# Turned tiles, first weight loads, exponentials and state rows: four small moves in the order of a one-core decoder step

## The chip, the cores and the metric

The kernel runs on one core of a Trainium2 chip. A core has five engines with instruction streams of their own: TensorE (PE in the profile, with its weight loads as PEld), VectorE (DVE), ScalarE (ACT), GpSimd (POOL) and SyncE (SP, which here only issues transfers). They meet through semaphores: an instruction waits until another engine or a transfer has counted a semaphore up. On-chip memory is SBUF, and the matmul results go to PSUM, which has eight banks here. The metric is the device time of one launch in microseconds. Over three runs the kernel before takes 994.75 us (median; 994.54 to 995.33). Smaller is better.

## What is computed

One step of a decoder layer over a prompt of 512 tokens and eight samples of four tokens (544 token columns together), with a model width of 1024:

```python
h = rmsnorm(x, norm_mix_pre)
xr, q, k, v, g = split(h @ w_in)              # 1024 x 4608
A = rg_lru(causal_conv4(xr))                  # r, i = sigmoid(block-diagonal products)
                                              # a = exp(log_a), mult = sqrt(1 - a*a), linear scan
B = sliding_window_attention(q, k, v)         # 8 heads, 2 kv heads, sinks, relative bias
m = (sigmoid(gA) * (A @ w_lru_o) + sigmoid(gB) * (B @ w_attn_o)) @ w_out
x = x + rmsnorm(m, norm_mix_post)
u = causal_conv3(rmsnorm(x, norm_ffn_pre) @ w_up)          # 1024 x 8192
x = x + rmsnorm((gelu(u_gate) * u_val) @ w_down, norm_ffn_post)
```

Besides x it returns the states: the last recurrent rows, the last keys and values, and the last two rows of `h @ w_up` for the prompt and for each sample (`p_ffn_conv` and `s_ffn_conv`).

## The kernel before, in words

Activations lie turned: channels on the 128 partitions, tokens along the free axis, in eight tiles `k` of 128 channels. A product in single precision is made of three matmuls on operands split into a high and a low part (`hH`, `hL` and `wh`, `wl`): high by high, low by high, high by low. The 544 columns are done in two halves, 256 and 288 columns wide (`HALF`). PE runs one long list of such products in the order of the program text; ACT and DVE run an order written out by hand too. What is not a product (splits of weights, gates, scans, norms, outgoing rows) hangs on a clock of the program: `now[0]` counts a tick for each product step, `start_at(t, generator)` puts side work on a tick, `last` and `late` hold work that is queued at the end of a tick or in the next one. In the second part of the kernel (up and down projections) `slot()` does the same in steps of half a unit.

**The start (L377 to L497).** SP issues the first loads in the order of the text: the first token tiles with the two halves of the first weight tile (L384 to L387), the second weight tile (`wload(1)`), the small `relx` and `ohp`, the token tile 2, the third weight tile (`wload(2)`), token tiles 3 and 4, and the fourth and fifth weight tiles (L388 to L398). Each weight tile is 512 KB. `turn_a(z)` (L467) turns the first 256 token columns of channel tiles 4z to 4z+3 by TensorE transposes into PSUM; `hsplit` makes `hH` of them on ACT and `hL` on DVE; `first_mm` feeds them to the first product. A PSUM bank has room for two such turned tiles of 256 columns. Before the change a bank holds the neighbours 2kk and 2kk+1, and the loop takes the tiles in the order 0, 2, 1, 3, 4, 6, 5, 7 (L480). `keep_a` (L504) copies the turned tiles into SBUF later, `norms` (L554) puts these copies on their ticks, `turn_b` turns the other 288 columns, and `roots` and `spread_roots` make the row `rep` of reciprocal roots.

**The mixer's ticks (L79 to L81, used around L1045 to L1115).** For each of the eight recurrent channel tiles, `GATES` names the tick of the gate products and their sigmoids (`rg`, `ig`), `EXPS` the tick of a Tanh and an Exp (`th`, then `rg` at L994) and `SCANS` that of the scan. The attention gates `ga` get their sigmoids (`gate_later`, L1091) from tick GATES[0] + c + 1 on. A weight split is an ACT copy of 512 columns (`wh_...`, L283) and a DVE subtraction (`wl_...`, L290). How many weights ahead of its product a step splits depends on its tick against `GATES[3]` and `GATES[7]` (the argument `look`, L1109 and L1113). Channels 4 to 7 have ticks 73 to 76 in GATES, and L1111 decides which of the gates `gl` have their sigmoid late.

**The end (L1714 to L1930).** The last eighth of the down projection (four F tiles, group `QL`) works on the second column half in `for c in range(8): down(QL, c, 1, ...)` (L1892). Each such tile is 12 matmuls of 288 columns into one of three PSUM banks (`PM`), then a DVE addition into `ft` (L1815), a square on ACT (`sq_sum`, `sq_ft` in the profile, L1180) and a DVE addition into `acc`; the last square goes to `sq7`. At c = 5 ACT makes a warming Sqrt, which loads the table of that function (L1895). After the eight, PE takes held tiles of the group before, on the first column half; between the first and the second of them `stats` multiplies `acc` and `sq7` with ones (`pst_o`, six and six matmuls of one column). `x1_again` (L1716) turns a saved token tile back in four pieces (`px`), which ACT copies into `xtok`. `ffn_states` (L1731) turns the rows of the ffn state: eight transposes into `pfs` and `pfp`, an ACT copy of each into `ffn_rows_s` and `ffn_rows_p` (L1741, L1742), and a POOL transfer of each to the output; this twice, one time unit (two slots) apart. It starts three units after the plan's eighth tile from the end, `x1_again` one unit after it, with its first turned piece at four.

**The shared buffers.** `S(...)` draws from a pool of 53 SBUF tiles (`S_BUFS`, L46). A tile that has been read for the last time gives its buffer to a later one, and the first writer of that later one waits for that last reading; where this is a transfer to the output, it waits until the transfer has landed. When the last eight down tiles run, these S tiles are read until the end: `ft` (8), `x1r` (8, read in `finish_b`), the high and low F tiles 24 to 31 (16), the split weights `dl` (16: four k, two kk, high and low), and, once written, `xtok` (4): 52 in all. The rows of the ffn state (four tiles of S) come beside them.

The lines that set the state rows' tiles and their place:

```python
            o1, o2 = S(f"ffn_rows_s{kk}"), S(f"ffn_rows_p{kk}")
            act.copy(o1[:, 0:512], px)
            act.copy(o2[:16, 0:512], py[:16, :])
            pool.dma_start(out=os_[:, kk * 512:(kk + 1) * 512], in_=o1[:, 0:512])
...
            start_at(now[0] + 1, x1_again())
            start_at(now[0] + 3, ffn_states())
```

Of the kernel before, what the change touches and what calls it, by code (L numbers as in the profile page):

```python
# [17 lines left out]
P = 128  # L18
D = 1024
KD = D // P  # L20
# [55 lines left out]
KEEP = 3  # L76
FILL = 1
TURNED = 8
GATES = (51, 53, 55, 57, 73, 74, 75, 76)  # L79
EXPS = (58, 59, 60, 61, 78, 79, 80, 81)  # L80
SCANS = (62, 63, 65, 67, 82, 83, 85, 86)  # L81


def _bucket(d):
# [39 lines left out]
def hawk_step(ctx, tc, I, O):  # L124
    nc = tc.nc
    act, dve, pool, pe = nc.scalar, nc.vector, nc.gpsimd, nc.tensor
# [28 lines left out]
    def PX(name):  # L155
        return psx.tile([P, 512], F32, tag="aux", name=name)
# [24 lines left out]
    side, now, serial, late, last, mids, after, taps = [], [0], [0], [], [], [], [], []  # L181

    def start_at(t, gen):
        serial[0] += 1
        side.append([t, serial[0], gen])
# [34 lines left out]
    ident = keep.tile([P, P], F32, name="ident")  # L220
# [7 lines left out]
    def wsrc(key):  # L228
        kind = key[0]
        if kind in ("wr", "wi"):  # L230
            return I["lru_" + kind][0, 4 * key[1]:4 * key[1] + 4].rearrange("n c d -> c n d")
        w = {"in": w_in, "lo": I["w_lru_o"][0], "ao": I["w_attn_o"][0], "out": I["w_out"][0]}[kind]
        c = key[-1]
        return w[:, c * P:(c + 1) * P].rearrange("(k p) n -> p k n", p=P)
# [13 lines left out]
    def wname(i):  # L248
        return "_".join(str(z) for z in order[i])

    def wload(i):
        key = order[i]
        raw = wraw[i] = rp.tile([P, KD, P], F32, tag="raw", name="raw_" + wname(i))
        if key[0] == "wg":
            for z, nme in enumerate(("lru_wr", "lru_wi")):
                nc.sync.dma_start(out=raw[:, 4 * z:4 * z + 4, :],
                                  in_=I[nme][0, 4 * key[1]:4 * key[1] + 4].rearrange("n c d -> c n d"))
        else:
            nc.sync.dma_start(out=raw, in_=wsrc(key))
# [11 lines left out]
    def wsplit_hi(un, eng=None):  # L271
        i, u = un // 2, un % 2
        hl = []
        for x in "hl":
            if order[i] in in_slots:
                t_ = S(f"w{x}{u}_{wname(i)}", F32R)[:, 0:512]
                t_ = t_.rearrange("p (k n) -> p k n", k=4)
            else:
                t_ = wp.tile([P, 4, P], F32R, tag="w", name=f"w{x}{u}_{wname(i)}")
            hl.append(t_)  # L280
        raw = wraw[i][:, 4 * u:4 * u + 4, :]
        if eng is None:
            act.activation(hl[0], raw, AF.Copy)  # L283
        else:
            eng.tensor_copy(hl[0], raw)
        wunits[un] = hl
        return raw, hl
# [89 lines left out]
    def xload(i, halves=(0, 1)):  # L377
        t0, n, src = TOK[i]
        for z in halves:
            xt[i, z] = S(f"x{i}_{z}")  # L380
            nc.sync.dma_start(out=xt[i, z][:n, 0:512], in_=src[:, 512 * z:512 * z + 512])

    raw0 = wraw[0] = rp.tile([P, KD, P], F32, tag="raw", name="raw_" + wname(0))
    for z in range(2):  # L384
        xload(0, (z,))
        xload(1, (z,))
        nc.sync.dma_start(out=raw0[:, 4 * z:4 * z + 4, :], in_=wsrc(order[0])[:, 4 * z:4 * z + 4, :])  # L387
    wload(1)  # L388
    relx = cp.tile([NBK, NH], F32, name="relx")
    nc.sync.dma_start(out=relx, in_=I["rel_bias"])  # L390
    ohp = T("ohp")[:NBK, 0:WIN]
    nc.sync.dma_start(out=ohp, in_=I["c_ohp"])
    xload(2)
    wload(2)
    xload(3)
    xload(4)
    wload(3)
    wload(4)  # L398
    for r, nme in ((8, "norm_mix_post"), (16, "norm_ffn_pre"), (24, "norm_ffn_post")):
        nc.sync.dma_start(out=rows_a[r:r + 8, :], in_=I[nme].rearrange("o (k p) -> (o k) p", p=P))  # L400
# [46 lines left out]
    def xtile(i, k):  # L447
        n = TOK[i][1]
        return xt[i, k // 4][:n, (k % 4) * P:(k % 4 + 1) * P]

    def hsplit(k, a, ps):
        g = pv[:, G_PRE + k:G_PRE + k + 1]
        act.activation(h.get(k, a, 0), ps, AF.Copy, scale=g)
        stt(h.get(k, a, 1), ps, g, f32(h.get(k, a, 0)), ALU.mult, ALU.subtract)
# [4 lines left out]
    u0, u1 = wclaim(2)  # L459
    first_ps = PM("pm_first")  # L460

    def first_mm(k, i0, i1, start=False, stop=False):
        mm(first_ps[:, :256], wunits[k // 4][i0][:, k % 4, :], h.get(k, 0, i1), start, stop)

    ps_ta = []

    def turn_a(z):  # L467
        for kk in (2 * z, 2 * z + 1):
            ps_ta.append(PX(f"ps_ta{kk}"))
            for q in range(4):  # L470
                pe.transpose(ps_ta[-1][:, q * P:(q + 1) * P], xtile(q % 2, 2 * kk + q // 2), ident)

    def first_low(z):
        for k in range(4 * z, 4 * z + 4):
            first_mm(k, 1, 0, stop=k == KD - 1)

    turn_a(0)
    for z in range(FILL):
        dummy(z)
    ks = (0, 2, 1, 3, 4, 6, 5, 7)  # L480
    for q, k in enumerate(ks):
        if q in (0, 4):
            raw, hl = wsplit_hi((u0, u1)[q // 4], eng=dve)
        hsplit(k, 0, ps_ta[k // 2][:, k % 2 * 256:k % 2 * 256 + 256])
        if q in (0, 4):
            wsplit_lo(raw, hl, eng=pool)
        first_mm(k, 0, 0, start=q == 0)
        if q not in (0, 4):
            first_mm(ks[q - 1], 0, 1)
        if q == 2:  # L490
            turn_a(1)
        if q == 3:
            first_mm(k, 0, 1)
            first_low(0)
    first_mm(ks[-1], 0, 1)
    first_low(1)
    xsquare(1, 1, False)  # L497

    xn = [S(f"xn{k}") for k in range(KD)]
# [2 lines left out]
    tb = []  # L502

    def keep_a(k):  # L504
        act.copy(xn[k][:, 0:256], ps_ta[k // 2][:, k % 2 * 256:k % 2 * 256 + 256])

    def keep_b(k, ps):
        (dve.tensor_copy if k % 4 > 1 else act.copy)(xn[k][:, 256:NT], ps[:, :288])
# [45 lines left out]
    def norms():  # L554
        xsquare(0, 1, True)
        yield from roots(0, 2)
        yield
        last.extend(lambda k=k: keep_a(k) for k in range(6))
        last.append(lambda: xsquares(2))
        yield  # L560
        turn_b(range(4))
        last.extend(lambda k=k: keep_a(k) for k in (6, 7))
        yield
        turn_b(range(4, KD))
        last.extend(lambda i=i: xsquares(i) for i in (3, 4))
        yield
        yield from roots(2, 5)
        dve.tensor_scalar(rq, ss[:, 1, 0:4], SCALE, None, ALU.mult)
# [488 lines left out]
    for c in range(8):  # L1057
        start_at(GATES[c], gates(c))
        start_at(EXPS[c], lru_exp(c))
        start_at(SCANS[c], lru_scan(c))  # L1060

# [32 lines left out]
    for c in range(8):  # L1094
        for a in range(2):
            step(("in", 28 + c), h, a, gate_done(sg, c, "ga", True), look=1 if now[0] + 1 >= GATES[0] else 2)
        start_at(GATES[0] + c + 1, once(gate_later, sg, c))
        for a in range(2):
            step(("in", c), h, a, lambda a, ps, c=c: xr_done(c, a, ps), look=1 if now[0] + 1 >= GATES[0] else 2)

# [6 lines left out]
    for c in range(8):  # L1107
        for a in range(2):
            step(("ao", c), A, a, ao_done(c), look=1 if now[0] + 1 <= GATES[3] + 2 else 2)  # L1109
    for c in range(8):  # L1110
        raw = 75 + 2 * c > GATES[7] + 1 and c < 7  # L1111
        for a in range(2):
            step(("in", 20 + c), h, a, gate_done(gl, c, "gl", raw), look=1 if now[0] + 1 <= GATES[7] + 2 else 2)  # L1113
        if raw:
            start_at(SCANS[7] + c - 1, once(gate_later, gl, c))  # L1115
    start_at(now[0] + 8, lru_states())
# [614 lines left out]
    def ffn_states():  # L1731
        os_ = O["s_ffn_conv"].rearrange("o b i (m n) -> (o b i m) n", n=D)
        op = O["p_ffn_conv"].rearrange("o b i (m n) -> (o b i m) n", n=D)
        for kk in range(2):
            px = PX(f"pfs{kk}")
            py = PX(f"pfp{kk}")
            for j in range(4):
                pe.transpose(px[:, j * P:(j + 1) * P], sfT[:, 4 * kk + j].rearrange("p r m -> p (r m)"), ident)
                pe.transpose(py[:16, j * P:(j + 1) * P], stage_p[:, 4 * kk + j].rearrange("p r m -> p (r m)"), ident)
# [4 lines that stand above are left out]
            pool.dma_start(out=op[:, kk * 512:(kk + 1) * 512], in_=o2[:16, 0:512])  # L1744
            yield
# [17 lines left out]
    for i, x in enumerate(plan):  # L1763
        more[0] = min(4, max(0, i - len(plan) + LASTS))
        if x[0] == "s":
            pair(*x[1:])
            slot()
        elif x[0] == "q":
            plain(*x)
            slot(x[3])  # L1770
        else:
            _, q, c, a = x
            down(q, c, a, down_done(q, c))
            slot(a)
        if i == len(plan) - 8:
            start_at(now[0] + 1, x1_again())
            start_at(now[0] + 3, ffn_states())

    yp, ys = O["y_p"][0], O["y_s"].rearrange("b t d -> (b t) d")
    sq7 = {}  # L1780
# [194 lines left out]
```

## Time and profile before

| | value |
|---|---|
| median of three runs | 994.75 us (994.54 to 995.33) |
| the profiled execution's own time | 994.97 us |
| its span, first to last instruction | 993.2 us |
| PE busy | 983.9 us, 99% of the span |
| DVE busy | 746.6 us, 75% |
| ACT busy | 566.5 us, 57% |
| POOL busy | 160.4 us, 16% |
| mean granted TensorE clock | 0.998 |

A row of the timeline reads: start in us from the span's beginning, duration, engine, line of the program, operation, output from input, shape, count of neighbours put together, and in brackets the idle time of that engine before it with what ended it. The table of waits lists, by engine, what was waited for, the sum in us, how often, and the longest. PE's matmuls overlap: one of 256 columns is listed with 0.28 us, while the next one starts sooner than that, so times on PE are read from start to start.

### The profile page before, as it was taken

To read this page: it belongs to the slowest core of one execution; us is meant where nothing else is said; L and a number is where in the kernel's file an instruction comes from. 1 tells how busy PE (TensorE), PEld (TensorE's weight loads), DVE (VectorE), ACT (ScalarE), POOL (GpSimd) and SP (SyncE) were. 2 spreads that over 40 slices of the span, in tenths; PEclk is the share of its full clock that TensorE was granted. 3 is DMA by queue.
4 is the path that set the end of the run, shared out by engine and by line. 5 is a ranking of instruction groups with operands and counts; after the bars stand their busy time and mean duration, and the time that the engine had idled before them with its cause. 6 is when DMAs were issued, how large, how long until landed. Compare 5 with 4: busy or idle time off the path is not lost.

```text
span 993.2 us, 20120 instructions
## 1 busy us (share of the span) xinstructions
PE 983.9 (99%) x7783; PEld 972.7 (98%) x7783; DVE 746.6 (75%) x1609; ACT 566.5 (57%) x1362; POOL 160.4 (16%) x269
## 2 busy tenths in 40 slices
PE   9999999999999999999999999999999999999997
PEld 8999999999999999999999999999999999999996
DVE  5777677766948655589776788888888888888766
ACT  6544433468557535556776655555655555556652
POOL 2062000001504441210001010101010101011004
PEclk9999999999999999999999999999999999999999
DMA  7765222332322535236147676777777777768612
GB/s 209 185 218 185 68 86 86 107 86 80 91 85 86 189 104 144 64 112 196 41 117 165 154 160 160 159 161 158 162 156 163 156 163 156 164 147 204 196 47 90
DMA packets 210999, 135.62 MB, mean 137 GB/s; under 512 B 8845, under 2 KB 197021, under 8 KB 210872
## 3 DMA queue, kind: packets, MB, share of 16 engines
q1 hardware_dynamic: 198920, 112.72, 40.1%
q0 software_dynamic: 11920, 19.59, 11.9%
q10 hardware_dynamic: 64, 2.04, 0.5%
q8 instruction: 61, 1.00, 0.4%
q14 instruction: 34, 0.28, 0.1%
HBM read 111.78 MB, written 11.37 MB: 124 GB/s over the span
## 4 chain that ended last, share of the span: by engine, by line
PE 93%; ACT 2%; DVE 2%; DMA 1%; issue 0%; SPq 0%; DVEq 0%; ACTq 0%
PE pmin L165 21%; PE pmdn L165 17%; PE pux L1524 16%; PE puy L1524 8%; PE pq L1524 6%; PE pmout L165 5%; PE pmlo L165 5%; PE puz L1524 4%; PE pmao L165 4%; DMA raw_in<-in_w_in_dram 1%; PE psc L165 1%; PE pvp L165 1%; PE pg L165 1%; PE ptok L165 1%; PE pt L817 1%
## 5 line engine op out<-in xcount | busy, mean ns | idle before, releaser
L165 PE MATMUL pmin<-hH,wh_in 128*128 128x256 f32 (+1 forms) x568 | 165.2, 293 | 0.2 <-ACT wh_in L283 0.2
L165 PE MATMUL pmin<-hL,wh_in 128*128 128x256 f32 (+1 forms) x568 | 162.8, 289 | 0.0
L165 PE MATMUL pmin<-hH,wl_in 128*128 128x256 f32 (+1 forms) x568 | 158.7, 287 | 0.0
L165 PE MATMUL pmdn<-fH,wh_dn 128*128 128x256 f32 (+1 forms) x448 | 129.2, 288 | 0.2 <-DVE ft L174 0.2
L165 PE MATMUL pmdn<-fL,wh_dn 128*128 128x256 f32 (+1 forms) x448 | 129.0, 288 | 0.0
L165 PE MATMUL pmdn<-fH,wl_dn 128*128 128x256 f32 (+1 forms) x448 | 128.9, 288 | 0.0
L177 DVE SCALAR_TENSOR_TENSOR uc<-u,fv,uc 128x560 f32<-128x560 f32 x128 | 102.0, 797 | 13.3 <-ACT uc L1555 13.2
L165 PEld LDWEIGHTS pmin<-hH,wh_in 128*128 128x128 f32 x568 | 106.9, 188 | 1.9 <-issue 1.2
L165 PEld LDWEIGHTS pmin<-hL,wh_in 128*128 128x128 f32 x568 | 107.1, 189 | 0.1
L165 PEld LDWEIGHTS pmin<-hH,wl_in 128*128 128x128 f32 x568 | 105.0, 188 | 0.2 <-issue 0.2
L165 PEld LDWEIGHTS pmdn<-fH,wh_dn 128*128 128x128 f32 x448 | 84.3, 188 | 0.6 <-issue 0.6
L165 PEld LDWEIGHTS pmdn<-fH,wl_dn 128*128 128x128 f32 x448 | 84.4, 188 | 0.0
L165 PEld LDWEIGHTS pmdn<-fL,wh_dn 128*128 128x128 f32 x448 | 84.3, 188 | 0.0
L1650 ACT COPY u<-pux 128x272 f32<-128x272 f32 x52 | 20.1, 387 | 83.9 <-PE pux L1524 83.8
L168 DVE TENSOR_TENSOR u<-puy,u 128x240 f32<-128x240 f32 (+2 forms) x78 | 24.6, 344 | 49.7 <-PE puy L1524 32.7
L283 ACT ACTIVATE wh_in<-raw_in 128x512 fp32r<-128x512 f32 x70 | 42.8, 628 | 29.8 <-issue 12.1
L174 DVE TENSOR_TENSOR ft<-ft,pmdn 128x256 f32<-128x256 f32 (+1 forms) x104 | 45.2, 436 | 17.1 <-PE pmdn L165 16.6
L290 DVE TENSOR_TENSOR wl_in<-raw_in,wh_in 128x512 fp32r<-128x512 f32 x70 | 48.1, 697 | 1.3 <-ACT wh_in L283 1.2
L1555 ACT ACTIVATE uc<-u,fv 128x560 f32<-128x560 f32 x64 | 48.2, 755 | 0.0
L1450 POOL DMA_DIRECT2D raw_up_s<-raw_up_s x26 | 22.7, 872 | 102.0 <-DMA raw_up_s<-raw_up__7496 4.7
L168 DVE TENSOR_TENSOR wl_dn<-raw_dn,wh_dn 128x512 fp32r<-128x512 f32 x56 | 38.4, 685 | 0.0
L165 PE MATMUL pmout<-mH,wh_out 128*128 128x272 f32 x128 | 37.4, 292 | 0.0
(779 smaller groups left out, 3390.0 us busy)
## 6 DMA issues: line engine op xcount, KB each, us to landing
raw_in<-in_w_in_dram SPq DMA_DIRECT2D x35, 512.0 KB
raw_dn<-in_w_down_dram SPq DMA_DIRECT2D x56, 256.0 KB
raw_up_s<-in_w_up_dram SPq DMA_DIRECT2D x25, 512.0 KB
raw_up_s<-raw_up_s POOLq DMA_DIRECT2D x26, 256.0 KB, 5.6
raw_ao<-in_w_attn_o_dram SPq DMA_DIRECT2D x8, 512.0 KB
raw_lo<-in_w_lru_o_dram SPq DMA_DIRECT2D x8, 512.0 KB
raw_out<-in_w_out_dram SPq DMA_DIRECT2D x8, 512.0 KB
xdram<-xn POOLq DMA_DIRECT2D x8, 272.0 KB, 7.5
```

Of the source, the lines that this page charges most:

```text
L165: pe.matmul(out, l, r, start=start, stop=stop)
L168: dve.tensor_tensor(out=out, in0=a, in1=b, op=ALU.subtract)
L174: dve.tensor_tensor(out=out, in0=a, in1=b, op=ALU.add)
L177: dve.scalar_tensor_tensor(out=out, in0=a, scalar=s_, in1=b, op0=op0, op1=op1)
L283: act.activation(hl[0], raw, AF.Copy)
L290: (eng or dve).tensor_tensor(out=hl[1], in0=raw, in1=f32(hl[0]), op=ALU.subtract)
L817: pe.transpose(pt[:, (2 * ch + j) * P:(2 * ch + j + 1) * P], s3[:, j, ch * P:(ch + 1) * P], ident)
L1450: pool.dma_start(out=w["p4"], in_=w["p2"], accum_op=ALU.add)
L1524: pe.matmul(ps[:, :HN], w, x, start=start and k == 0 and i == 0, stop=stop and k == 3 and i == 2, skip_group_check=True)
L1555: act.activation(yt[j][:, 0:FLATU], u[:, 0:FLATU], AF.Copy, scale=fv[:, j:j + 1])
L1650: act.copy(e[nm_], z)
```

## The change

Four parts. First, a PSUM bank of the first turned columns now holds the channel tiles k and k+4, so that the four banks are all begun by the first turn and completed by the second; the loop takes the tiles in plain order, and the first low product of a tile is queued after the second turn. The copies in `norms` are taken in the order 0, 4, 1, 5, 2, 6, and then 3, 7. Second, the third weight tile is loaded ahead of `relx` and `ohp`, and the fourth ahead of token tiles 2, 3 and 4. Third, the exponentials of the first four recurrent channel tiles come at ticks 60 to 63 instead of 58 to 61, their scans at 64, 65, 67, 69 instead of 62, 63, 65, 67, and the gates of the last four one tick earlier, with the test for `raw` adjusted so that it picks the same tiles. Fourth, the ffn state's rows start five time units after the marked tile instead of three, which is four slots later.

```diff
-GATES = (51, 53, 55, 57, 73, 74, 75, 76)
-EXPS = (58, 59, 60, 61, 78, 79, 80, 81)
-SCANS = (62, 63, 65, 67, 82, 83, 85, 86)
+GATES = (51, 53, 55, 57, 72, 73, 74, 75)
+EXPS = (60, 61, 62, 63, 78, 79, 80, 81)
+SCANS = (64, 65, 67, 69, 82, 83, 85, 86)
...
     wload(1)
+    wload(2)
     relx = cp.tile([NBK, NH], F32, name="relx")
     nc.sync.dma_start(out=relx, in_=I["rel_bias"])
     ohp = T("ohp")[:NBK, 0:WIN]
     nc.sync.dma_start(out=ohp, in_=I["c_ohp"])
-    xload(2)
-    wload(2)
-    xload(3)
-    xload(4)
     wload(3)
+    for i in (2, 3, 4):
+        xload(i)
     wload(4)
...
     def turn_a(z):
-        for kk in (2 * z, 2 * z + 1):
-            ps_ta.append(PX(f"ps_ta{kk}"))
-            for q in range(4):
-                pe.transpose(ps_ta[-1][:, q * P:(q + 1) * P], xtile(q % 2, 2 * kk + q // 2), ident)
+        for k in range(4 * z, 4 * z + 4):
+            if not z:
+                ps_ta.append(PX(f"ps_ta{k}"))
+            for q in range(2):
+                pe.transpose(turned_a(k)[:, q * P:(q + 1) * P], xtile(q, k), ident)
+
+    def turned_a(k):
+        return ps_ta[k % 4][:, k // 4 * 256:k // 4 * 256 + 256]
...
-    ks = (0, 2, 1, 3, 4, 6, 5, 7)
-    for q, k in enumerate(ks):
-        if q in (0, 4):
-            raw, hl = wsplit_hi((u0, u1)[q // 4], eng=dve)
-        hsplit(k, 0, ps_ta[k // 2][:, k % 2 * 256:k % 2 * 256 + 256])
-        if q in (0, 4):
+    for k in range(KD):
+        if k % 4 == 0:
+            raw, hl = wsplit_hi((u0, u1)[k // 4], eng=dve)
+        hsplit(k, 0, turned_a(k))
+        if k % 4 == 0:
             wsplit_lo(raw, hl, eng=pool)
-        first_mm(k, 0, 0, start=q == 0)
-        if q not in (0, 4):
-            first_mm(ks[q - 1], 0, 1)
-        if q == 2:
+        first_mm(k, 0, 0, start=k == 0)
+        if k == 3:
             turn_a(1)
-        if q == 3:
+        if k % 4:
+            first_mm(k - 1, 0, 1)
+        if k % 4 == 3:
             first_mm(k, 0, 1)
+        if k == 3:
             first_low(0)
-    first_mm(ks[-1], 0, 1)
     first_low(1)
...
-        last.extend(lambda k=k: keep_a(k) for k in range(6))
+        last.extend(lambda k=k: keep_a(k) for k in (0, 4, 1, 5, 2, 6))
...
-        raw = 75 + 2 * c > GATES[7] + 1 and c < 7
+        raw = 75 + 2 * c > GATES[7] + 2 and c < 7
...
-            start_at(now[0] + 3, ffn_states())
+            start_at(now[0] + 5, ffn_states())
```

More of the change, by code (lines that the diff above doesn't have):

```diff
@@ L504, in keep_a @@
     def keep_a(k):
-        act.copy(xn[k][:, 0:256], ps_ta[k // 2][:, k % 2 * 256:k % 2 * 256 + 256])
+        act.copy(xn[k][:, 0:256], turned_a(k))
     def keep_b(k, ps):
@@ L561, in norms @@
         turn_b(range(4))
-        last.extend(lambda k=k: keep_a(k) for k in (6, 7))
+        last.extend(lambda k=k: keep_a(k) for k in (3, 7))
         yield
```

## The prediction

> **What bounds the kernel now.** I read the page first, then PE's table of waits, then timelines of each engine around the four places that the change touches. The page and the table:
>
> ```profile
> PE   9999999999999999999999999999999999999997
> ```
>
> ```profile
> PE pmdn L165 <- ACT ffn_rows_s L1741: 0.4, 1, 0.4
> ...
> PE pmao L165 <- DVE wl_ao L290: 0.2, 1, 0.2
> ...
> PE pmao L165 <- ACT wh_ao L283: 0.2, 1, 0.2
> ```
>
> PE is busy in every slice, so an edit off PE counts only where PE stands still for it. The waits at the edited places are a few tenths each: little can be won here, while what can be lost is not bounded by them. A listed wait is also only a part of its stall, because the first matmul behind one is stretched; I go by start times. The stall at the attention output (`pmao`):
>
> ```profile
> 241.64 0.28 PE L165 MATMUL pmao<-aH,wh_ao 128*128 128x256 f32 x1
> ...
> 242.23 0.28 PE L165 MATMUL pmao<-aH,wl_ao 128*128 128x256 f32 x1
> ...
> 243.62 0.28 PE L165 MATMUL pmao<-aH,wh_ao 128*128 128x256 f32 x1
> ```
>
> Five matmuls, from 241.64 to 242.23, are 0.118 us apart. The next four, to 243.62, took 1.39 where 0.47 was due: 0.92 is lost here.
>
> **Exponentials two ticks later.** Why those weights were late stands in ACT's timeline (first and last of the five table loads of this stretch, and the copies between), and the busy time of DVE (third engine) in a window of 22 us:
>
> ```profile
> 231.28 1.28 ACT L994 ACT_TABLE_LOAD   x1
> ...
> 241.97 1.68 ACT L283 ACTIVATE wh_ao<-raw_ao 128x512 fp32r<-128x512 f32 x3
> ...
> 244.34 1.28 ACT L994 ACT_TABLE_LOAD   x1
> ```
>
> ```profile
> 227.00:249.00 22.00, 21.60 (x170) 21.20 (x169) 13.68 (x23) 21.80 (x34) 4.78 (x8) 1.00 0.30 89
> ```
>
> ACT is busy for 21.80 of these 22 us, and five table loads of 1.28 are in it: the exponentials at ticks 58 to 61 lie between sigmoids at ticks up to 59, and each change of function reloads the table. The weight copies behind them come late, three at once at 241.97. With all four exponentials at 60 or later the sigmoids are through first, and one load does for five: 4 x 1.28 = 5.1 us less on ACT. That is several times the stall, so I take -0.92, the nearest row; bounds: nothing, if four exponentials in a row only move the late copies to the next weight, and -0.92. The scans two ticks later go to DVE, busy 13.68 of 22 here, which covers them. Gates 4 to 7 one tick earlier fall where the table lists no wait of PE. I price both at nothing, and if that cover goes, at another wait of the 0.2 kind in the table.
>
> **Loads and turned tiles.** The fourth weight tile's load is a piece of the chain that ended last (start, duration):
>
> ```profile
> 11.80 6.77 DMA raw_in<-in_w_in_dram
> ```
>
> DVE, ACT and PE in the timeline:
>
> ```profile
> 10.53 0.88 DVE L177 SCALAR_TENSOR_TENSOR hL<-ps_ta,pv,hH 128x256 fp32r<-128x256 f32 x2 [0.15 <-ACT hH L453]
> ...
> 10.97 1.15 ACT L283 ACTIVATE wh_in<-raw_in 128x512 fp32r<-128x512 f32 x2
> ...
> 14.40 1.15 ACT L283 ACTIVATE wh_in<-raw_in 128x512 fp32r<-128x512 f32 x2 [0.78 <-DMA raw_in<-in_w_in_dram]
> 18.02 0.37 ACT L547 COPY rep<-ps_rep 128x256 f32<-128x256 f32 x1 [2.47 <-PE ps_rep L165]
> 18.60 1.15 ACT L283 ACTIVATE wh_in<-raw_in 128x512 fp32r<-128x512 f32 x2 [0.20 <-DMA raw_in<-in_w_in_dram]
> ...
> 14.40 0.74 PE L165 MATMUL pmin<-hH,wl_in 128*128 128x256 f32 x5
> ...
> 15.31 0.29 PE L165 MATMUL pmin<-hL,wh_in 128*128 128x256 f32 x1
> ...
> 17.92 1.21 PE L165 MATMUL pmin<-hH,wl_in 128*128 128x256 f32 x8
> ...
> 19.50 0.28 PE L165 MATMUL pmin<-hL,wh_in 128*128 128x256 f32 x1
> ```
>
> ACT waits for the third weight tile until 14.40 and for the fourth (issued 11.80, landed 18.57) until 18.60. On PE six matmuls from 14.40 to 15.31 took 0.91 where 0.71 was due, and nine from 17.92 to 19.50 took 1.58 where 1.06 was due. Ahead of `relx`, `ohp` and the later tokens both tiles land some microseconds sooner. The first loss, 0.20, goes. Of the second, the copy of `rep` ends at 18.39 and the weight's copy can follow it instead of starting at 18.60: 0.2 goes, and `rep` is late next. Moved back on SP's queue are the two small loads and three token tiles; the tiles' reader on PE, `turn_b`, comes behind the product of 19.50, and nothing reads them before. Were that cover gone, PE would wait about as long as the load between them takes, at worst some 2 us.
>
> With k and k+4 in one bank, `hL` of a tile no longer alternates with `hH` of its neighbour: the 0.15 at 10.53 goes. The second weight's copy starts at 10.97 in any case, so not much more can: -0.1, bounds nothing and -0.3. The start gives 0.1 + 0.2 + 0.2 = 0.5 (bounds nothing and 0.9).
>
> **State rows four slots later.** This part decides. PE, then ACT, then POOL's issue and the landing of `ffn_rows_s` (the two of them, from issue):
>
> ```profile
> 951.38 0.27 PE L1738 MATMUL pfs<-ident,sfT 128*128 128x128 f32 x1
> ...
> 952.03 0.27 PE L1738 MATMUL pfs<-ident,sfT 128*128 128x128 f32 x1
> ...
> 952.17 0.38 PE L165 MATMUL pmdn<-fH,wh_dl 128*128 128x288 f32 x1
> ...
> 958.70 0.38 PE L165 MATMUL pmdn<-fH,wh_dl 128*128 128x288 f32 x1
> ...
> 967.59 0.81 PE L165 MATMUL pst_o<-ones,sq 128*128 128x1 f32 x6
> ```
>
> ```profile
> 948.63 0.56 ACT L1741 COPY ffn_rows_s<-pfs 128x512 f32<-128x512 f32 x1
> ...
> 952.34 0.59 ACT L1741 COPY ffn_rows_s<-pfs 128x512 f32<-128x512 f32 x1 [0.18 <-PE pfs L1738]
> ...
> 960.43 1.28 ACT L1895 ACT_TABLE_LOAD   x1
> ...
> 961.84 0.43 ACT L1180 ACTIVATE sq_ft<-ft 128x288 f32<-128x288 f32 x1
> 963.15 0.44 ACT L1180 ACTIVATE sq_ft<-ft 128x288 f32<-128x288 f32 x1 [0.89 <-DVE ft L174]
> ```
>
> ```profile
> 949.49 0.58 POOL L1743 DMA_DIRECT2D out_dram<-ffn_rows_s  x1 [20.57 <-ACT ffn_rows_s L1741]
> ```
>
> ```profile
> DMA to landing us min/median/max: 2.4/2.8/3.3
> ```
>
> Of the 53 S buffers 48 are held to the end, and 52 once the four `xtok` stand. Where the rows run now, one `xtok` is there (its piece is turned just ahead of 951.38): 48 + 1 + 4 rows = 53, which fits exactly. Four slots later the first pair of rows comes with the third `xtok` and the second pair behind the fourth: 52 + `ffn_rows_s1` fill the pool, and `ffn_rows_p1` finds only the buffer of `ffn_rows_s1`. Its copy then waits until that transfer has landed. ACT runs in order, and behind that copy stand the table load and the last four squares, for which `acc`, the `ft` additions behind it on DVE, and PE's held tile wait.
>
> In this trace's time: the second group of eight transposes (0.79 us, 951.38 to 952.17) now follows the down tile that begins at 958.70. Its place stays empty and the first group comes into PE's path instead, so that tile moves by about +0.1. Twelve matmuls of 0.134 end at 960.4; the last `pfs` starts 0.65 into its group (951.38 to 952.03), its copy 0.31 later, at 961.34. The issue of the transfer is 0.86 behind the copy's start (948.63 to 949.49): 962.2. Landing takes 2.4 to 3.3 us from there. I take 2.4, since this one runs alone while the second one before ran beside the load of `gpost`: 964.6. Then the copy of `ffn_rows_p1`, 0.59 like the one at 952.34, and from 965.2 the table load. The first square comes 1.41 behind that load as now (960.43 to 961.84), at 966.6 instead of 961.84, and each further one 1.31 behind the last (961.84 to 963.15: square, addition to `acc`, addition to `ft`). The fourth starts at 970.5 and ends at 971.0, so the second half of `pst_o` starts at 971.1 instead of 967.59: **+3.5**. Everything behind it on PE follows. Bounds: nothing, where no buffer is short, and +4.4 with a landing of 3.3. POOL has only small work behind these transfers.
>
> [...]
>
> **Sum.** 994.97 - 0.92 - 0.5 + 3.5 = 997.05 for a profiled execution. The profiled one stood 0.22 above the median of its runs, so 996.8; because the landing can only take longer than the shortest one seen, I forecast **996.9**. The main case's own range, gains of 0.6 to 1.6 against a loss of 3.2 to 4.6: 996.1 to 998.7.
>
> **Rivals.** *The rows move freely* (the other side): buffers suffice, the eight transposes stay hidden, and PE's wait for `ffn_rows_s` goes.
>
> ```profile
> 948.59 0.30 PE L165 MATMUL pmdn<-fH,wl_dn 128*128 128x288 f32 x1
> 949.26 0.38 PE L165 MATMUL pmdn<-fH,wh_dl 128*128 128x288 f32 x1 [0.38 <-ACT ffn_rows_s L1741]
> ```
>
> ```profile
> 948.67 0.45 DVE L174 TENSOR_TENSOR ft<-ft,pmdn 128x288 f32<-128x288 f32 x1
> ```
>
> That wait is 0.54 from start to start (0.67 against 0.13), so 994.75 - 0.92 - 0.5 - 0.54 = 992.8. The bracket speaks for it. Against it: the copy had begun at 948.63, and what ended shortly before 949.26 is the `ft` addition (949.12), which frees a PSUM bank. It decides if a 54th tile is never alive when `ffn_rows_p1` is written.
>
> *Visible transposes, no buffer wait*: the wait of 949.26 stays, and 0.8 us of transposes that now lie in other waits come into PE's path: 994.75 - 1.42 + 0.8 = 994.1. It also stands for a wait on a buffer that other idle time of ACT hides.
>
> *The clock falls.* In the main case PE idles some 1.5 us ahead of the held tile and again around `pst_o`. One window at the run's end (the third number from its end is PE's granted clock), and PE's first and last matmuls:
>
> ```profile
> 989.00:990.00 1.00, 0.00 (x0) 0.00 (x0) 0.00 (x0) 0.00 (x0) 0.00 (x0) 0.57 1.03 356
> ```
>
> ```profile
> 1.00 2.50 PE L165 MATMUL ps_warm<-ones 128*128 128x128 f32 x10 [1.00 <-POOL ones L219]
> ...
> 5.08 1.54 PE L471 MATMUL ps_ta<-ident,x 128*128 128x128 f32 x8
> ...
> 986.25 0.71 PE L1803 MATMUL pyo<-ident,ft 128*32 128x128 f32 x5
> ```
>
> The last matmul ended at 986.96, and the mean clock of 0.57 from 989 to 990 means a fall soon after 989: some 2 us of idleness did it, more than either gap. Ten matmuls of 128 columns took 2.50 from 1.00 on, and eight from 5.08 on still 1.54, against 0.79 for the eight above; PE was slow for some 5 us from its first matmul. Half of that is +2.5: 999.4. [...]
>
> **How the numbers follow.** Main case 0.72, transposes only 0.12, free rows 0.08, clock 0.08. Two tenths of a per cent, 2.0 us here, is what a measurement of this kernel tells from no change: the same lies between 992.8 and 996.7. Free rows lie on its lower edge; I give faster 0.07 with what the start may add. Within the main case I give six in ten to above 996.7, with the clock 0.08 + 0.43 = 0.51 slower; the rest, 0.42, is the same. The range 993.8 to 998.9 leaves out the free rows and the clock.
>
> **What would show it.** Right: one table load on ACT between 231 and 246 instead of five, and `pmao` without the 0.92; the third and fourth weight's copies at about 13.7 and 18.2; `ffn_rows_p1` copied some 3.3 us behind `ffn_rows_s1` with ACT idle between, the four squares 4.7 later, and a listed wait of PE for `ft` and for `pst_o`'s inputs. The prediction is wrong if the second pair is copied without that gap, or if work of ACT, DVE and PE behind it can be done in another order than I have it.

## The result and the profile after

The changed kernel takes 997.51 us (median of eight executions, 996.46 to 999.85), the one before 995.09 us in the same comparison (994.50 to 995.42). The ratio is 1.0029, with a 95% interval of 1.0018 to 1.0040: slower by 0.3%. The forecast was 996.9 in 993.8 to 998.9.

The eight times are not one cloud. Four lie at 996.46 to 996.81, each with a mean granted clock of 0.999; I call these the undisturbed ones. Four lie at 998.21, 998.48, 999.51 and 999.85, with clocks of 0.995 to 0.998. The median is the midpoint between the two groups (996.81 and 998.21), a time that no execution took. Four executions in the experiments below stand far apart without an explanation (1187.14, 1366.59 and 5468.66 us of variants, 2465.97 of the kernel before) and are left out of the medians and ranges given there.

The profiled execution, 998.21 us with a span of 996.4, is one of the second group, so its trace shows both things that the change costs. PE's table of waits of the kernel after, in the form in which the one before was shown:

```profile
span 996.4 us, 20123 instructions
```

```profile
PE pmdn L165 <- DVE ft L174: 2.3, 3, 1.3
PE pm_first L165 <- DVE wh_in L285: 1.2, 1, 1.2
...
PE pst_o L165 <- DVE acc L174: 0.6, 1, 0.6
...
PE pmdn L165 <- ACT wh_dl L1463: 0.4, 1, 0.4
```

The two waits at `pmao` and the one at `pmin` (0.2, for `wh_in`) are gone; two at the end of the down projection are new, 1.3 and 0.6 us. (The 1.2 at `pm_first` ends with the cast `wh_in` of the first weight tile, which itself waits for the tile's landing; in the kernel before the table listed 0.3 there, for `hH`. The first product begins at 7.24 here and at 7.12 before.) Where the two new waits come from stands in ACT's timeline of the kernel after:

```profile
957.96 0.59 ACT L1729 COPY xtok<-px 128x512 f32<-128x512 f32 x1 [1.97 <-DMA out_dram<-ffn_rows_s]
...
959.58 0.59 ACT L1743 COPY ffn_rows_s<-pfs 128x512 f32<-128x512 f32 x1 [0.21 <-ACT frow L1585]
962.84 0.57 ACT L1744 COPY ffn_rows_p<-pfp 16x512 f32<-16x512 f32 x1 [2.68 <-DMA out_dram<-ffn_rows_s]
963.43 1.28 ACT L1897 ACT_TABLE_LOAD   x1
...
964.84 0.43 ACT L1182 ACTIVATE sq_ft<-ft 128x288 f32<-128x288 f32 x1
966.15 0.44 ACT L1182 ACTIVATE sq_ft<-ft 128x288 f32<-128x288 f32 x1 [0.89 <-DVE ft L174]
...
968.82 0.44 ACT L1177 ACTIVATE sq<-ft 128x288 f32<-128x288 f32 x1 [0.89 <-DVE ft L174]
```

ACT stands idle for 2.68 us before the copy of the second prompt rows, and the bracket names the releaser: the transfer of the sample rows. ACT's later squares all follow it. The first row shows that the pool was full even earlier: the fourth `xtok` waits 1.97 us for the landing of the first sample rows. The prediction did not have this wait; it is over before the second rows are turned (958.57 to 959.36), so it delays nothing here. The landing of these transfers (2.3 us both) and what PE makes of it:

```profile
DMA to landing us min/median/max: 2.3/2.3/2.4
```

```profile
966.17 0.39 PE L165 MATMUL pmdn<-fH,wh_dn 128*128 128x256 f32 x1 [1.34 <-DVE ft L174]
...
968.47 0.83 PE L165 MATMUL pst_o<-ones,acc 128*128 128x1 f32 x6 [0.62 <-DVE acc L174]
969.31 0.83 PE L165 MATMUL pst_o<-ones,sq 128*128 128x1 f32 x6
...
970.44 0.41 PE L165 MATMUL pmdn<-fH,wh_dn 128*128 128x256 f32 x1
970.65 0.41 PE L165 MATMUL pmdn<-fL,wh_dn 128*128 128x256 f32 x1
...
973.63 0.38 PE L165 MATMUL pmdn<-fH,wh_dn 128*128 128x256 f32 x1
```

Two readings. First, set the same instructions of both kernels side by side. The tile whose matmul waits at 945.27 here (the row stands with the first experiment) was at 947.06 before:

```profile
947.06 0.37 PE L165 MATMUL pmdn<-fH,wh_dn 128*128 128x288 f32 x1
```

So this execution is 1.79 us ahead when it reaches the rows. The second half of `pst_o` is at 969.31 here and was at 967.59 before: 1.72 behind. Between the two places it loses 1.79 + 1.72 = 3.5 us. Second, from 970.44 the matmuls of 256 columns are 0.21 us apart instead of 0.118. That is the clock, in windows of 2 us (third number from the end):

```profile
968.00:970.00 2.00, 1.52 (x12) 1.43 (x13) 0.78 (x2) 0.44 (x1) 0.00 (x0) 1.00 0.00 0
970.00:972.00 2.00, 2.00 (x13) 2.00 (x13) 1.38 (x9) 0.26 (x1) 0.00 (x0) 0.61 0.00 0
972.00:974.00 2.00, 2.00 (x12) 2.00 (x12) 0.72 (x2) 0.00 (x0) 0.00 (x0) 0.54 0.00 0
974.00:976.00 2.00, 2.00 (x13) 1.72 (x12) 0.87 (x3) 0.00 (x0) 0.27 (x1) 1.00 0.00 0
```

PE works without a pause here, but at about half speed, for some 3.4 us (970.44 to about 973.8), and is another 1.5 us late afterwards (spans: 996.4 - 993.2 = 3.2 = -1.8 + 3.5 + 1.5). A page that gives busy shares does not show it: a slow matmul counts as busy (PE has 2.00 of 2.00 us in the windows at 0.61 and 0.54).

Of the start and of the gates, ACT's timeline of the kernel after:

```profile
13.32 1.14 ACT L283 ACTIVATE wh_in<-raw_in 128x512 fp32r<-128x512 f32 x2
...
17.89 1.16 ACT L283 ACTIVATE wh_in<-raw_in 128x512 fp32r<-128x512 f32 x2
...
235.05 1.66 ACT L283 ACTIVATE wh_ao<-raw_ao 128x512 fp32r<-128x512 f32 x3
...
237.39 1.28 ACT L996 ACT_TABLE_LOAD   x1
...
247.06 1.28 ACT L1006 ACT_TABLE_LOAD   x1
```

One load for the exponentials (237.39), the next only for the roots, and the weight copies 7 us earlier than before (235.05 instead of 241.97). The third and fourth weight's copies at the start wait for no transfer any more.

### The profile page after: what moved, and what is told of

It is laid out like the page before. It is cut to its first block, busy times and chain, and to the rows that moved or that the text cites. A ratio compares the mean times of both kernels' runs of the same rounds, so it can differ in the third digit from the quotient of the medians.

```text
span 996.4 us, 20123 instructions
## 1 busy us (share of the span) xinstructions
PE 984.2 (99%) x7783; PEld 973.6 (98%) x7783; DVE 745.8 (75%) x1609; ACT 561.3 (56%) x1358; POOL 160.6 (16%) x269
## 4 chain that ended last, share of the span: by engine, by line
PE 93%; issue 4%; DVE 2%; DMA 1%; ACT 0%; POOL 0%; SPq 0%; DVEq 0%; ACTq 0%; POOLq 0%
PE pmin L165 22%; PE pmdn L165 16%; PE pux L1526 15%; PE puy L1526 8%; PE pq L1526 6%; PE pmout L165 5%; PE pmao L165 5%; PE pmlo L165 5%; PE puz L1526 4%; PE pg L165 1%; PE psc L165 1%; PE pvp L165 1%; PE ptok L165 1%; PE pt L819 1%; DMA raw_in<-in_w_in_dram 0%
```

## The experiments

**The rows alone put back.** The changed kernel, with the state rows at their old place:

```diff
-            start_at(now[0] + 5, ffn_states())
+            start_at(now[0] + 3, ffn_states())
```

> The changed kernel with the state rows back at three units (as before), all else as changed. Theory (the copy of the second prompt rows waits for a buffer, and that wait is the whole loss): the trace of the changed kernel stands 1.8 us ahead of the one before at the place of the rows, so about 995.1 - 1.8 = 993.3 us, range 992.7 to 993.8, no run above 994, granted clock 0.998 or more, no copy on ACT waiting for a transfer. Rival (the loss comes from the other parts, or the rows cost PE their eight transposes wherever they stand): 995.5 or more.

Measured: 992.93 us (992.63 to 993.49, eleven executions) beside 994.69 for the kernel before; ratio 0.9981, interval 0.9972 to 0.9990. So the other three parts together are a gain of 1.76 us, and the rows are the whole loss. This version is faster than both kernels. PE's wait that the table ascribes to the rows is there, as in the kernel before:

```profile
947.45 0.37 PE L165 MATMUL pmdn<-fH,wh_dl 128*128 128x288 f32 x1 [0.39 <-ACT ffn_rows_s L1743]
```

and the same matmul in the changed kernel, where the rows come some 9 us later:

```profile
945.27 0.37 PE L165 MATMUL pmdn<-fH,wh_dn 128*128 128x288 f32 x1 [0.81 <-DVE ft L174]
947.48 0.38 PE L165 MATMUL pmdn<-fH,wh_dl 128*128 128x288 f32 x1 [0.39 <-ACT wh_dl L1463]
```

The wait is as long (0.39) without the rows and gets another name. The eight transposes that filled PE ahead of the tile before it have left a wait for `ft` (0.81) in their place. So moving the rows away frees nothing here.

**The rows alone moved.** The kernel before, with only this line:

```diff
-            start_at(now[0] + 3, ffn_states())
+            start_at(now[0] + 5, ffn_states())
```

> The kernel before with the state rows alone moved to five units. Theory: +3.5 for the buffer wait, so 998.6 us in executions whose clock holds, and up to 3 us more in those whose clock falls; median 998.4 to 1000.5; the copy of ffn_rows_p1 some 3.3 us behind that of ffn_rows_s1, ACT idle for about 2.7 us on the transfer. Rival (only the transposes become visible): 995.1 + 0.8 = 995.9.

Measured: 999.83 us (998.36 to 1000.02, five executions) beside 994.69; ratio 1.0046, interval 1.0033 to 1.0058. Its lowest time is 3.7 above the median of the kernel before, the others 4.8 to 5.3. Its profile, of the execution at 999.83, shows a low clock as well (0.52 in the window 972 to 974, 0.63 in 974 to 976). ACT in this kernel:

```profile
961.24 0.59 ACT L1741 COPY ffn_rows_s<-pfs 128x512 f32<-128x512 f32 x1 [0.20 <-ACT frow L1583]
964.53 0.58 ACT L1742 COPY ffn_rows_p<-pfp 16x512 f32<-16x512 f32 x1 [2.71 <-DMA out_dram<-ffn_rows_s]
```

The second copy is 3.29 behind the first. The visible transposes alone (995.9) are ruled out.

**The rows late, with buffers for all.** What makes the copy wait is taken away: the prompt rows come from another pool.

```diff
-            o1, o2 = S(f"ffn_rows_s{kk}"), S(f"ffn_rows_p{kk}")
+            o1, o2 = S(f"ffn_rows_s{kk}"), T(f"ffn_rows_p{kk}")
```

> The changed kernel, rows as late as there, but the two tiles of the prompt rows come from the pool of temporaries instead of the 53 S buffers. Theory (buffer wait): the 2.7 us wait of ACT goes, the gap of PE behind the last down tile and the one at pst_o go with it, and what stays of the late place is at most the eight transposes: 993.3 to 994.2 us, no clock fall. Rival (the place itself costs, as the rows stand among squares and down tiles): 996 or more.

Measured: 994.00 us (993.54 to 994.61, eleven executions); ratio to the kernel before 0.9992, interval 0.9983 to 1.0001. ACT and PE in this kernel:

```profile
959.38 0.59 ACT L1743 COPY ffn_rows_s<-pfs 128x512 f32<-128x512 f32 x1 [0.99 <-ACT frow L1585]
959.86 0.57 ACT L1744 COPY ffn_rows_p<-pfp 16x512 f32<-16x512 f32 x1
960.45 1.28 ACT L1897 ACT_TABLE_LOAD   x1
...
965.91 0.72 PE L165 MATMUL pst_o<-ones,acc 128*128 128x1 f32 x6
966.49 0.81 PE L165 MATMUL pst_o<-ones,sq 128*128 128x1 f32 x6
```

The second copy follows the first directly, PE has no gap at `pst_o`, and the time falls by 3.5 us from the changed kernel's median (by 2.8 from the middle of its four undisturbed executions; by 2.4 if each is first compared with the kernel before of its own comparison, 995.09 and 994.69). The buffer was the cause. The late place itself costs 994.00 - 992.93 = 1.1 us. The eight transposes that now stand in PE's path (958.57 to 959.36 in the changed kernel's trace) are 0.79 of it; the rest is not accounted for.

**PE's gaps filled.** The four next runs ask what lets the clock fall. They are the changed kernel, waits and all, with matmuls of ones that nothing reads; each is two passes of 0.109 us on PE (in the first run's trace 24 from 964.41 to 967.00 and 10 from 968.50 to 969.61). The first, with n = 12 and m = 5; a second with n = 5 and m = 2; then only the first place (n = 5), and only the second (m = 2):

```diff
+    fill = PX("ps_fill")
+
+    def fill_in(n):
+        for z in range(n):
+            mm(fill[:, z % 4 * P:z % 4 * P + P], ones, ones, True, True)
+
+    fill_in(n)
     for _, q, c, a in held:
         down(q, c, a, down_done(q, c))
+        if c == HELD:
+            fill_in(m)
         slot(0)
```

> The changed kernel with 12 matmuls of ones (128 columns) on PE in the gap behind the last down tile and 5 in the gap ahead of pst_o; their results are not used, and the waits stay. Theory (PE's two gaps, 1.3 and 0.6 us, close together, let the clock fall in about half of the executions): the time becomes that of the undisturbed ones, 996.4 to 997.0 us, all of them within 0.5 us, granted clock 0.999 in every one. Rival (the clock falls for another reason, or its fall is not what spreads the times): the times spread from 996.5 to 999.9 as in the changed kernel.

Measured with 12 and 5: 997.53 to 998.30 us in six executions, median 997.75. I had counted one pass for each matmul, so 24 and 10 passes overfill the gaps, and the forecast of 996.4 to 997.0 was missed by about the surplus. The spread shrank from 3.4 to 0.8 us.

> The changed kernel with fewer matmuls of ones in PE's gaps, 5 and 2 (each is two passes of 0.109 us, so 1.1 and 0.4 us, less than the gaps of 1.5 and 0.9). Theory (idle time on PE lets the clock fall): no execution with a fallen clock, 996.4 to 997.0 us with a spread below 0.6, as the undisturbed half of the changed kernel. Rival: some executions at 998 to 1000 again.

Measured with 5 and 2: 996.65 us (996.13 to 997.10, eleven executions). That is the level of the changed kernel's undisturbed half, and no execution lies at 998 or more; the spread of 1.0 is more than the 0.6 expected. The clock in its profile is 1.00 in every window from 962 to 978.

> The changed kernel with matmuls of ones (5, ten passes) only in PE's first gap, behind the last down tile. Theory A (the two gaps together let the clock fall): none of the executions falls, 996.4 to 997.1 us. Theory B (the thin stretch around pst_o alone does it): some executions at 998 to 1000. Theory C (the first gap alone does it): as A here, but falls in the run beside it, where that gap is open.

Measured with only the first gap filled: 997.86 us, two of eight executions at 996.28 and 996.67, six at 997.50 to 998.90. The windows of this kernel's profile (of the execution at 998.16) show the low clock:

```profile
968.00:970.00 2.00, 1.55 (x13) 1.46 (x13) 0.75 (x2) 0.44 (x1) 0.00 (x0) 1.00 0.00 0
970.00:972.00 2.00, 2.00 (x15) 2.00 (x16) 1.41 (x9) 0.27 (x1) 0.00 (x0) 0.83 0.00 0
972.00:974.00 2.00, 2.00 (x12) 2.00 (x11) 0.60 (x2) 0.00 (x0) 0.00 (x0) 0.50 0.00 0
```

> The changed kernel with matmuls of ones (2, four passes) only in PE's second gap, ahead of pst_o. Theory A (both gaps together): no fall, 996.4 to 997.1 us. Theory B (the stretch around pst_o alone): no fall. Theory C (the first gap of 1.5 us alone): some executions at 998 to 1000.

Measured with only the second filled: 996.90 us; nine of eleven executions at 996.48 to 997.23, two at 997.74 and 997.98. PE in its profile (of the execution at 996.52, with a clock of 1.00 in every window from 962 to 978):

```profile
966.01 0.38 PE L165 MATMUL pmdn<-fH,wh_dn 128*128 128x256 f32 x1 [1.33 <-DVE ft L174]
...
967.53 0.61 PE L165 MATMUL ps_fill<-ones 128*128 128x128 f32 x4
968.31 0.83 PE L165 MATMUL pst_o<-ones,acc 128*128 128x1 f32 x6 [0.17 <-DVE acc L174]
```

So the longer gap of 1.3 us may stay open with hardly a fall, while the shorter one at `pst_o` makes most executions fall. Theories A and C do not fit, and B is left: it is the stretch around `pst_o`, an empty 0.6 to 0.8 us and then twelve matmuls of one column. Except in the profiled executions, a fall is inferred from the time, and that is not a sure sign: single executions of the kernel before, which has no such gap, came at 996.42 and 996.79 too, about 2 us above its median, with a mean clock of 0.999. So whether the two at 997.74 and 997.98 fell is open, as they have no profile.

**The other parts one by one**, each alone in the kernel before (the ticks, the loads, the turned tiles, each with its lines of the change, shortened here):

```diff
-GATES = (51, 53, 55, 57, 73, 74, 75, 76)
-EXPS = (58, 59, 60, 61, 78, 79, 80, 81)
-SCANS = (62, 63, 65, 67, 82, 83, 85, 86)
+GATES = (51, 53, 55, 57, 72, 73, 74, 75)
+EXPS = (60, 61, 62, 63, 78, 79, 80, 81)
+SCANS = (64, 65, 67, 69, 82, 83, 85, 86)
...
-        raw = 75 + 2 * c > GATES[7] + 1 and c < 7
+        raw = 75 + 2 * c > GATES[7] + 2 and c < 7
```

> The kernel before with the ticks of gates, exponentials and scans alone as changed. Theory: one table load on ACT instead of five between 231 and 246, the stall of 0.92 at the attention output gone and the two small ones behind it (0.2 and 0.1) too: 0.9 to 1.2 less, 993.5 to 993.8 us beside 994.7. Rival (late weight copies only move on): no change, 994.6 or more.

```diff
     wload(1)
+    wload(2)
...
-    xload(2)
-    wload(2)
-    xload(3)
-    xload(4)
     wload(3)
+    for i in (2, 3, 4):
+        xload(i)
```

> The kernel before with the order of the first loads alone as changed. Theory: 0.4 less (0.20 at the third weight tile, 0.2 at the fourth), 994.3 us; the third weight's copy on ACT begins before 14.0, the fourth's right behind the copy of rep. Rival (the loads are hidden or cost the later tokens): 994.7 or more.

```diff
-        for kk in (2 * z, 2 * z + 1):
-            ps_ta.append(PX(f"ps_ta{kk}"))
...
+    def turned_a(k):
+        return ps_ta[k % 4][:, k // 4 * 256:k // 4 * 256 + 256]
...
-    ks = (0, 2, 1, 3, 4, 6, 5, 7)
-    for q, k in enumerate(ks):
+    for k in range(KD):
```

> The kernel before with the turned tiles alone as changed (k and k+4 in a bank). Theory: 0.1 to 0.3 less, 994.4 to 994.6 us, hL of tiles 4 to 7 on DVE without a wait. Rival: nothing or a loss, since the later loads set the pace, 994.7 or more. Together with the two runs beside it the differences must add up to that of the changed kernel with early rows, -1.76.

| part alone | median us | ratio to before (95%) |
|---|---|---|
| kernel before | 994.71 | |
| ticks | 993.19 (992.96 to 994.06) | 0.9987 (0.9978 to 0.9995) |
| loads | 994.61 (994.19 to 995.01) | 0.9997 (0.9989 to 1.0006) |
| turned tiles | 994.63 (994.11 to 994.91) | 0.9998 (0.9989 to 1.0007) |

The medians' differences are -1.52, -0.10 and -0.08, together -1.70 beside the -1.76 of the first experiment. All three missed the times expected: the ticks gained more, the loads and the turned tiles less. The ticks are a gain clear of noise; of the loads and the turned tiles, neither alone can be told from nothing. For the ticks the profile has two table loads where six were (five of the exponentials' stretch, one for the roots):

```profile
237.79 1.28 ACT L994 ACT_TABLE_LOAD   x1
247.47 1.28 ACT L1004 ACT_TABLE_LOAD   x1
```

The loads' run does show its mechanism: the third weight's copy begins at 13.68 and the fourth's right behind `rep`. But in the ticks' run, whose loads are those of before, the same copies stand at

```profile
13.74 1.15 ACT L283 ACTIVATE wh_in<-raw_in 128x512 fp32r<-128x512 f32 x2 [0.28 <-DMA raw_in<-in_w_in_dram]
17.66 0.37 ACT L547 COPY rep<-ps_rep 128x256 f32<-128x256 f32 x1 [2.76 <-PE ps_rep L165]
17.98 1.16 ACT L283 ACTIVATE wh_in<-raw_in 128x512 fp32r<-128x512 f32 x2
```

instead of 14.40 and 18.60. So when these copies can begin differs from one execution to the next by about as much as I had counted as the loss.

## Why the prediction was right, and where it was not

**The buffer wait** was right in mechanism and size. Forecast: landing 2.4, copies 3.3 apart, the squares' step 1.31, +3.5 at `pst_o`. Shown: landing 2.3 to 2.4, copies 3.26 apart (959.58, 962.84), 1.31 (964.84 to 966.15), +3.5. Of these 3.5, the experiments give 1.1 to the late place and the rest to the buffer. That the transfer would be at the short end was right, and one even landed 0.1 sooner than the shortest seen before; that running alone is the reason was not tested.

**The wait that stays** (0.38 on `ffn_rows_s`) was right: without the rows it is 0.39 under another name. The free-rows rival (992.8) is out, and so is the one of visible transposes alone (994.1): with a buffer for every row the late place gives 994.0, and without one it is 2.4 to 2.8 us above that.

**The exponentials** were right in mechanism; the size was a little low. -0.92 was the stall at `pmao`; the part alone measured -1.52, with an interval of about -0.5 to -2.2. In the changed kernel's trace the two smaller stalls behind it (0.2 at 253.8 and 0.1 at 257, from start times before) are gone too, so 1.2 of it has a place. I had let them recur. The part moves the scans and the later gates too, and these were not tried apart; but the time that PE loses between 226 and 262, 1.2 us before, is gone in the trace of the ticks' run, in which one table load stands where five were.

**The start** is a term that was mis-sized, and the one least understood. I took -0.5 from one execution's waits. Loads and turned tiles alone gave -0.10 and -0.08, both within noise, while the copies that wait for the landings begin 0.6 us sooner or later from one execution to the next. Of the stall only what recurs in every execution can be won. The traces add something. The first matmul into `pk`, with which the start is over, is at 44.88 in the kernel before. It comes 0.65 to 0.97 us sooner in the seven profiles with both parts, 0.25 and 0.33 sooner with one of them, and 0.27 and 0.62 sooner in the two that, like the kernel before, have neither. Together the parts may thus win some 0.5 at the start, as forecast. But all seven lose about 0.4 again between the first matmul of `pux` and the last of `puz` (514.75 and 928.82 before; 512.50 and 926.99 with the rows put back), while the ticks' run does not. Why is open.

**The clock** is the step that failed. I gave its fall 0.08, as a case of its own beside the main one, arguing that some 2 us of idleness made it fall at the run's end and that both gaps would be shorter. In fact, by their times and mean clocks, half of the changed kernel's executions had it (seen directly only in the profiled one). The argument compared empty gaps only. The stretch that does it, 967.7 to 970.0, holds 0.6 us of nothing and twelve one-column matmuls listed as busy. The price, forecast as +2.5, was 1.5 in the profiled execution and, if the fall is all that slows them, up to about 3 in the slowest ones (999.85 against 996.8), which have no profile. The two cases come together rather than exclude each other, which puts the median of 997.51 above the 996.9 that the undisturbed half (996.46 to 996.81) comes close to.

**Luck** is in that closeness. The gains were 1.76 instead of the 1.42 of the sum, and the kernel before stood at 995.09 in this comparison, 0.34 above the 994.75 that I had counted from; the two errors cancel. That the median fell between the groups at 997.51 rests on their being four and four. And the main case's own range was added up wrongly: gains of 0.6 to 1.6 and a loss of 3.2 to 4.6 on 994.75 give 996.35 to 998.75, not 996.1 to 998.7.

## What to carry to other kernels

Count the live tiles of a pool before moving anything that draws on it: here the late rows found a full pool, and a harmless move became a wait of 2.68 us for a transfer. ACT ran nothing in that time, and the wait was paid by what was queued behind it: seven instructions of ACT, then DVE, then PE. A releaser in brackets is the last one listed and need not be the cause (0.39 us on `ffn_rows_s` became 0.39 us on `wh_dl` when the rows were away): before moving it away, ask what else ends at the same moment. And when a change opens a pause on PE next to very small matmuls (here 0.6 to 0.8 us beside twelve of one column, and by their times and clocks four of eight executions were slowed), take the fall of the clock as part of the main case, and look for it in matmul spacing (0.21 us instead of 0.118 here) and in several executions' times, since busy shares hide it (2.00 of 2.00 us at a clock of 0.54).

## What was not expected of the hardware

The clock fell after a stretch of about 2.3 us, in which PE was empty for 0.6 to 0.8 us and otherwise issued twelve matmuls of one column; a gap of 1.3 us with full matmuls on both sides hardly did it (two doubtful executions of eleven). In the kernel before, the same twelve small matmuls without the pause (967.00 to 968.26) leave the clock at full (from 968.58 on the matmuls keep their 0.12 us spacing):

```profile
964.00:968.00 4.00, 4.00 (x36) 4.00 (x34) 1.46 (x4) 0.97 (x3) 0.00 (x0) 1.00 0.00 0
969.00:972.00 3.00, 3.00 (x24) 2.85 (x24) 1.92 (x9) 0.00 (x0) 0.00 (x0) 1.00 0.00 0
```

By their times, the fall came in half of the executions of the changed kernel, in six of eight with the first gap filled and in four of five with the rows alone moved. In two of the three profiles that have it the start can be read from the matmuls: it began only after full ones had run again for 0.4 and 1.3 us (at 970.44 after 970.00 in the changed kernel, at about 971.3 after 969.97 with the first gap filled). In windows of 2 us the clock falls short of full by 0.39 and 0.46 in the changed kernel, by 0.17, 0.50 and 0.18 with the first gap filled, and by 0.48 and 0.37 with the rows alone moved: 0.85 each time, from which I estimate a length of 3.4 us at half the clock (0.50 in the window 972 to 974 with the first gap filled). Why the fall lasts this long, and why it comes in some executions only, is not shown by any run here.
